# The first tile of W_v loaded and split in two halves of columns

## The chip, the cores and the metric

The kernel runs on one core of a Trainium2 chip. The metric is the device time of one execution in microseconds: before the change 311.23 us, the median of three runs that lie between 311.21 and 311.30 us. Its engines work side by side and wait for each other by semaphores: PE (matmul; its weight loads are listed apart as PEld), DVE and ACT (element-wise work), POOL, and SP, which here does nothing but issue loads and stores. Data move over 16 DMA engines that all queues share.

## The reference, cut to what matters

```
h = rms_norm(x, pre_g)                          # x: (1, 1024, 1024) float32
p = h @ W_in                                    # -> u_A | v_A | g_A | z_B | g_B, 512 columns each
A = gelu(u_A) * (W_s layer_norm(gelu(v_A)) + b_s) * silu(g_A)
B = fourier_mix(z_B) * silu(g_B)                # 2-D DFT over positions and channels, then W_f
y = concat[A, B] @ W_out
out = x + rms_norm(y, post_g)
```

The change touches only the start of the part `v = h @ W_v`, the product of x (scaled by pre_g; the row norm is applied later) with the second 512 columns of W_in.

## The kernel before, in words

float32 operands are kept accurate by splitting: every operand is written as a high part of reduced precision (type fp32r) plus the rest, and a product is three matmuls, high x high, low x high (of the weight's rest), high x low (lines 75 to 78, `mm3`). So a tile has to be loaded, its high part cast (ACT or DVE), and its low part subtracted (DVE) before the third matmul of a product can run. x comes transposed: `hh[kt]` and `hl[kt]` are high and low part of 128 input features (index kt, 0 to 7) by 1024 positions; `wvh`, `wvl` are those of the 128 x 512 tile kt of W_v. A chunk c is 128 positions; its product over all kt is accumulated in one PSUM bank `pv`. Seven chunks run together, tile kt after tile kt.

Loads are issued by SP one after the other in the order of the code: `head0` (138 KB: the gain vectors and the first 256 positions of x's tile 0), `wv0` (256 KB: tile 0 of W_v), `head` (384 KB: the other 768 positions of x's tile 0), then for kt = 1 the tile of W_v (line 125, written `wv`) and the tile of x (`xr1`, 512 KB, line 117; SP's list has the tile of W_v first), then kt = 2 and on.

Before any data are there, PE runs eight matmuls on a tile of ones (`warm`, lines 105 and 106), to be busy when the first product comes. Tile 0 is done by an own loop (lines 235 to 238) in three groups of chunks (0 and 1, 2 to 4, 5 and 6), since the chunks of x arrive in parts; within a group all matmuls of one term run, then those of the next. From kt = 1 on each chunk runs its three matmuls in turn (`v_step`, lines 239 to 241). PE executes in exactly the order of the code. The order on DVE, ACT and SP is made by the scheduler.

DVE casts tile 0 of W_v (line 72) and subtracts for its low part (73), makes the low part of x (135, three slices for tile 0), then does the same for tile 1; ACT makes the high part of x (134) and from tile 1 on also the high part of W_v (70).

Of the kernel before, what the change touches and what calls it, by code (L numbers as in the profile page):

```python
# [15 lines left out]
D = 1024  # L16
KT = D // P
EPS = 1e-6
WARM = 8
LOAD_HALF = 1  # L20
FOLD_AT = (0, 1, 3, 4, 5, 7, 8, 10)
WZ_AT = (2, 6)
# [8 lines left out]
def encoder_layer_kernel(  # L31
# [15 lines left out]
    nc = tc.nc  # L47
# [9 lines left out]
    def slot(name, shape=(P, 1024), dt=F32):  # L57
        return big.tile(list(shape), dt, tag="S", name=name, bufs=NS)
# [6 lines left out]
    def bank(name):  # L65
        return ps.tile([P, 512], F32, tag="ps", name=name)

    def split(src, hi, lo, hi_on_act=True):
        if hi_on_act:
            nc.scalar.copy(hi, src)  # L70
        else:
            nc.vector.tensor_copy(hi, src)
        nc.vector.tensor_tensor(lo, src, hi.bitcast(F32), op=ALU.subtract)  # L73

    def mm3(o, lh, ll, rh, rl, start, stop, **kw):
        nc.tensor.matmul(o, lh, rh, start=start, stop=False, **kw)  # L76
        nc.tensor.matmul(o, lh, rl, start=False, stop=False, **kw)  # L77
        nc.tensor.matmul(o, ll, rh, start=False, stop=stop, **kw)  # L78


    head = slot("head")
    wv0 = raw_slot("wv0")
    head0 = con.tile([P, 276], F32, name="head0")
    vec_sb = head0[:, 0:20]
    nc.sync.dma_start(head0, x0[:, 0:276])
    nc.sync.dma_start(wv0[:, 0:512], w_nat[1, 0])
    nc.sync.dma_start(head[:, 256:1024], x0[:, 276:1044])
    pre_g, ln_g, b_f, ln_b = (vec_sb[:, a:b] for a, b in ((0, 8), (8, 12), (12, 16), (16, 20)))

    ones = con.tile([P, P], F32, name="ones")  # L90
# [13 lines left out]
    warm = bank("warm")  # L104
    for i in range(WARM):
        nc.tensor.matmul(warm[:, 0:P], ones, ones, start=True, stop=True)
# [3 lines left out]
    hh, hl, wv = [], [], []  # L110
    wvh = quad("wvh", (P, 8, 512), F32R)
    for kt in range(KT):
        if kt == 0:
            xr, pg = head, pre_g[:, 0:1]
        else:
            xr = raw_slot(f"xr{kt}")
            nc.sync.dma_start(xr, xT[kt - 1])
            pg = pre_g[:, kt:kt + 1]
        if kt % 2 == 0:
            wr = wv0 if kt == 0 else raw_slot(f"wv{kt}")  # L120
            wv.append((wvh[:, kt:kt + 2], slot(f"wvl{kt}", (P, 2, 512), F32R)))
        wrv = wr.rearrange("p (k n) -> p k n", k=2)[:, kt % 2]
        wh, wl = (t[:, kt % 2] for t in wv[-1])
        if kt > 0:
            nc.sync.dma_start(wrv, w_nat[1, kt])
        h = slot(f"hh{kt}", dt=F32R)
        l = slot(f"hl{kt}", dt=F32R)
        hh.append(h)
        hl.append(l)
        if kt == 0:  # L130
            split(wrv, wh, wl, hi_on_act=False)
        for sl in ([slice(0, 256), slice(256, 640), slice(640, 1024)] if kt == 0 else [slice(0, 1024)]):
            src = head0[:, 20:276] if kt == 0 and sl.start == 0 else xr[:, sl]
            nc.scalar.activation(h[:, sl], src, AF.Copy, scale=pg)
            nc.vector.scalar_tensor_tensor(l[:, sl], src, pg, h[:, sl].bitcast(F32), op0=ALU.mult, op1=ALU.subtract)  # L135
        if kt > 0:
            split(wrv, wh, wl)

    def chunk(t, c):
        return t[:, c * P:(c + 1) * P]  # L140
# [40 lines left out]

    def v_step(pv, c, kt):
        wh, wl = (t[:, kt % 2] for t in wv[kt // 2])
        mm3(pv, chunk(hh[kt], c), chunk(hl[kt], c), wh, wl, kt == 0, kt == KT - 1)


    wz = []
# [44 lines left out]
        return wh, wl  # L232

    pvs = [bank(f"pv{c}") for c in range(7)]
    for cs in (range(2), range(2, 5), range(5, 7)):
        for term in range(3):
            for c in cs:
                nc.tensor.matmul(pvs[c], chunk((hl if term == 2 else hh)[0], c), wv[0][term == 1][:, 0], start=term == 0, stop=False)
    for kt in range(1, KT):
        for c in range(7):  # L240
            v_step(pvs[c], c, kt)
    with tc.manual_schedule(engines={mybir.EngineType.Activation}):
        stats()
        wq = [feature_load(0)]
        wz_load(0)
        const_load()
        for c in range(7):
            v_gelu(c, pvs[c])
        wq.append(feature_load(1))
        v_norm(0, 7)  # L250
        pv = bank("pv7")
        for kt in range(KT):
            v_step(pv, 7, kt)
        v_gelu(7, pv)
        v_norm(7, 8)
# [567 lines left out]
```

## Time and profile before

| | |
|---|---|
| median of the runs | 311.23 us |
| the profiled execution, its own time | 310.65 us |
| its span, first to last instruction | 308.6 us |
| PE busy | 301.3 us, 98% of the span |
| DVE, ACT, POOL busy | 229.8, 131.4, 22.9 us |
| moved by DMA | 42.42 MB, mean 137 GB/s |

The span leaves out 2.05 us of the profiled execution's own time, which lie around the program. An engine's busy time says little about who sets the end; for that there is the chain that ended last, which is followed back from the last instruction to whatever released each step, and the list of waits by engine. Matmuls are pipelined and their ends are modelled, so distances are read from start to start. In timelines "x2" joins neighbours of one kind; in brackets stands the idle time of the engine before a row and what ended it.

### The profile page before, as it was taken

What the parts mean: (1) busy time and instruction counts of PE and PEld (TensorE: products, weight loads), DVE (VectorE), ACT (ScalarE), POOL (GpSimd) and SP (SyncE); (2) the same over time, 40 slices, a digit from 0 to 9 for tenths busy, and PEclk for the clock granted to TensorE, in tenths of its full rate; (3) what the DMA queues carried; (4) which work ended last, traced back from release to release, by engine and by line L of the source; (5) the groups of instructions that cost most, each with busy time, mean ns of one, the idle gap of its engine ahead of it and who ended that gap; (6) DMA issues with size and microseconds to landing.
All of it is one profiled execution on the core that took longest, in us unless ns stands there. A gap on an engine that the chain in (4) does not pass through costs nothing.

```text
span 308.6 us, 3982 instructions
## 1 busy us (share of the span) xinstructions
PE 301.3 (98%) x1497; PEld 253.0 (82%) x1497; DVE 229.8 (74%) x429; ACT 131.4 (43%) x215; POOL 22.9 (7%) x29
## 2 busy tenths in 40 slices
PE   8999999999999999999999999999999999999992
PEld 7788888888888888888888888888888888888881
DVE  4880652579888989987345799655888898898764
ACT  4879476323231233243241334334555554433321
POOL 0000301010000000000000000001310302030210
PEclk9999999999999999999999999999999999999997
DMA  7999716024224151140020108326990163749373
GB/s 248 414 407 410 268 60 204 11 68 135 71 68 138 68 204 55 68 136 2 0 69 2 68 0 213 130 68 194 241 239 10 23 115 67 205 72 265 142 199 143
DMA packets 15427, 42.42 MB, mean 137 GB/s; under 512 B 1456, under 2 KB 1712, under 8 KB 15408
## 3 DMA queue, kind: packets, MB, share of 16 engines
q1 hardware_dynamic: 12880, 35.87, 32.9%
q0 software_dynamic: 2528, 6.30, 11.3%
q8 instruction: 12, 0.20, 0.3%
q14 instruction: 7, 0.06, 0.1%
HBM read 37.96 MB, written 4.20 MB: 137 GB/s over the span
## 4 chain that ended last, share of the span: by engine, by line
PE 95%; DMA 2%; DVE 1%; SPq 1%; ACT 0%; DVEq 0%; POOLq 0%; issue 0%; ACTq 0%
PE pf L77 14%; PE pf L76 14%; PE pf L78 14%; PE pz L285 7%; PE pv L78 4%; PE pv L77 4%; PE pv L76 4%; PE bb L78 4%; PE bb L76 4%; PE bb L77 4%; PE bc L78 2%; PE bc L77 2%; PE bc L76 2%; PE pg L442 2%; PE ba L76 2%; PE ba L78 2%
## 5 line engine op out<-in xcount | busy, mean ns | idle before, releaser
L78 PE MATMUL pv<-wvh,hl 128*128 128x512 f32 x57 | 22.6, 396 | 0.1
L77 PE MATMUL pv<-wvl,hh 128*128 128x512 f32 x57 | 22.5, 394 | 0.0
L70 ACT CAST fh<-sd 128x1024 fp32r<-128x1024 f32 x8 | 8.4, 1049 | 33.0 <-DVE sd L273 33.0
L76 PE MATMUL pv<-wvh,hh 128*128 128x512 f32 x57 | 22.4, 393 | 0.0
L458 ACT ACTIVATE t<-t 128x512 f32<-128x512 f32 x16 | 10.1, 631 | 24.5 <-DVE t L457 24.4
L541 POOL DMA_DIRECT2D wo<-in_w_out x6 | 7.2, 1210 | 174.8 <-DVE t L457 150.9
L457 DVE TENSOR_TENSOR t<-pf,R 128x512 f32<-128x512 f32 x16 | 11.0, 688 | 11.8 <-PE pf L78 11.7
L285 PE MATMUL pz<-wzh,fh 128*128 128x260 f32 x64 | 18.1, 283 | 0.0
L285 PE MATMUL pz<-wzh,fl 128*128 128x260 f32 x64 | 18.0, 281 | 0.0
L285 PE MATMUL pz<-wzl,fh 128*128 128x260 f32 x64 | 18.0, 281 | 0.0
L575 ACT CAST cq<-s 128x512 fp32r<-128x512 f32 x16 | 9.9, 619 | 16.9 <-DVE s L567 15.4
L657 ACT ACTIVATE jk<-y 128x512 f32<-128x512 f32 x12 | 7.6, 632 | 18.6 <-DVE y L730 7.0
L271 DVE TENSOR_TENSOR sd<-hs 128x384 f32<-128x384 f32 x16 | 14.5, 907 | 0.2
L73 DVE TENSOR_TENSOR fl<-sd,fh 128x1024 fp32r<-128x1024 f32 x8 | 9.8, 1224 | 5.2 <-ACT fh L70 5.1
L78 PEld LDWEIGHTS pv<-wvh,hl 128*128 128x128 f32 x57 | 10.7, 188 | 3.0 <-DVE hl L135 0.6
L77 PEld LDWEIGHTS pv<-wvl,hh 128*128 128x128 f32 x57 | 10.7, 188 | 2.5
L76 PEld LDWEIGHTS pv<-wvh,hh 128*128 128x128 f32 x57 | 10.7, 188 | 2.5
L451 ACT ACTIVATE mixA<-t 128x512 f32<-128x512 f32 x8 | 5.1, 632 | 18.1 <-DVE t L450 18.1
L450 DVE TENSOR_TENSOR t<-pf,R 128x512 f32<-128x512 f32 x8 | 5.5, 688 | 9.5 <-PE pf L78 9.5
L285 PEld LDWEIGHTS pz<-wzl,fh 128*128 128x128 f32 x64 | 12.1, 189 | 0.3
L285 PEld LDWEIGHTS pz<-wzh,fh 128*128 128x128 f32 x64 | 12.1, 189 | 0.3
L285 PEld LDWEIGHTS pz<-wzh,fl 128*128 128x128 f32 x64 | 12.1, 189 | 0.0
(383 smaller groups left out, 938.2 us busy)
## 6 DMA issues: line engine op xcount, KB each, us to landing
wo<-in_w_out SPq DMA_DIRECT2D x10, 512.0 KB, 4.6
xc<-in_x SPq DMA_DIRECT2D x8, 512.0 KB, 10.1
xr<-in_xT SPq DMA_DIRECT2D x7, 512.0 KB, 7.7
hs<-in_xT SPq DMA_DIRECT2D x7, 512.0 KB, 3.3
wo<-in_w_out POOLq DMA_DIRECT2D x6, 512.0 KB, 9.0
y<-in_x POOLq DMA_DIRECT2D x5, 512.0 KB, 5.2
out<-y SPq DMA_DIRECT2D x5, 512.0 KB, 3.0
wv<-in_w_nat SPq DMA_DIRECT2D x8, 256.0 KB, 7.0
```

The lines of the kernel that those rows point to most:

```text
L70: nc.scalar.copy(hi, src)
L73: nc.vector.tensor_tensor(lo, src, hi.bitcast(F32), op=ALU.subtract)
L76: nc.tensor.matmul(o, lh, rh, start=start, stop=False, **kw)
L77: nc.tensor.matmul(o, lh, rl, start=False, stop=False, **kw)
L78: nc.tensor.matmul(o, ll, rh, start=False, stop=stop, **kw)
L271: nc.vector.tensor_tensor(sd[:, i, 1:4], hv[:, 1:4], hv[:, 7:4:-1, ::-1], op=op)
L285: nc.tensor.matmul(pz[t][:, cs], l[:, i, t], r[:, cs], start=kt == 0 and i == 0 and j == 0, stop=kt == KT - 1 and i == 1 and j == 2, skip_ ...
L457: nc.vector.tensor_tensor(t, pf, R[:, sl], op=ALU.mult)
L458: nc.scalar.activation(t, t, AF.Silu)
L541: nc.gpsimd.dma_start(t, quarter(add, i), accum_op=ALU.add)
L575: nc.scalar.copy(t[:, 0], src)
L657: nc.scalar.activation(jk[:, 0:w], src, AF.Square, accum_out=ssq[c][:, j:j + 1])
```

## The change

`wv0` is loaded by two DMAs of 256 columns each and the rest of x's tile 0 by two DMAs of 256 and 512 columns, so that five loads stand where three stood. DVE casts and subtracts the first half of the W_v tile as before; the second half is cast by ACT and subtracted by DVE, after the first slice of x. The slices of x's tile 0 become 256, 256 and 512 columns (before 256, 384, 384). PE starts with chunks 0 and 1 by halves of W_v's columns, twelve matmuls of 256 columns; the groups after it are chunks 2 and 3, then 4 to 6. Six warming matmuls run in place of eight.

```diff
-WARM = 8
+WARM = 6
...
-    nc.sync.dma_start(wv0[:, 0:512], w_nat[1, 0])
-    nc.sync.dma_start(head[:, 256:1024], x0[:, 276:1044])
+    for c0 in (0, 256):
+        nc.sync.dma_start(wv0[:, c0:c0 + 256], w_nat[1, 0, :, c0:c0 + 256])
+    for c0, c1 in ((256, 512), (512, 1024)):
+        nc.sync.dma_start(head[:, c0:c1], x0[:, 20 + c0:20 + c1])
...
-            split(wrv, wh, wl, hi_on_act=False)
-        for sl in ([slice(0, 256), slice(256, 640), slice(640, 1024)] if kt == 0 else [slice(0, 1024)]):
+            split(wrv[:, 0:256], wh[:, 0:256], wl[:, 0:256], hi_on_act=False)
+        for sl in ([slice(0, 256), slice(256, 512), slice(512, 1024)] if kt == 0 else [slice(0, 1024)]):
             src = head0[:, 20:276] if kt == 0 and sl.start == 0 else xr[:, sl]
+            if kt == 0 and sl.start == 256:
+                split(wrv[:, 256:512], wh[:, 256:512], wl[:, 256:512])
...
-    for cs in (range(2), range(2, 5), range(5, 7)):
+    for term, half in ((0, 0), (1, 0), (0, 1), (2, 0), (1, 1), (2, 1)):
+        ws = slice(256 * half, 256 * half + 256)
+        for c in range(2):
+            nc.tensor.matmul(pvs[c][:, ws], chunk((hl if term == 2 else hh)[0], c), wv[0][term == 1][:, 0, ws], start=term == half == 0, stop=False, skip_group_check=True)
+    for cs in (range(2, 4), range(4, 7)):
```

SP's list from the start of the program, before (L85 to L87 are tile 0, L125 and L117 the tiles kt = 1 of W_v and x):

```order
L85 DMA head_69<-in_x 128x276
L86 DMA wv_68<-in_w_nat 128x512
L87 DMA head<-in_x 128x768
L125 DMA wv_68<-in_w_nat 128x512
L117 DMA xr_102<-in_xT 128x1024
```

and after the change (L127 and L119 are the old L125 and L117):

```order
L85 DMA head_69<-in_x 128x276
L87 DMA wv_68<-in_w_nat 128x256 x2
L89 DMA head<-in_x 128x256
L89 DMA head<-in_x 128x512
L127 DMA wv_68<-in_w_nat 128x512
L119 DMA xr_104<-in_xT 128x1024
```

The load of x's tile 1 moves from the fifth to the seventh place; what follows it is in the old order.

PE's list from the first product on, before (pv_186 and pv_187 are the banks of chunks 0 and 1):

```order
L238 MATMUL pv_186<-wvh,hh_92 128x512
L238 MATMUL pv_187<-wvh,hh_92 128x512
L238 MATMUL pv_186<-wvl_91,hh_92 128x512
L238 MATMUL pv_187<-wvl_91,hh_92 128x512
L238 MATMUL pv_186<-wvh,hl_93 128x512
L238 MATMUL pv_187<-wvh,hl_93 128x512
```

and after it (the same banks are now pv_188 and pv_189):

```order
L242 MATMUL pv_188<-wvh,hh_92 128x256
L242 MATMUL pv_189<-wvh,hh_92 128x256
L242 MATMUL pv_188<-wvl_91,hh_92 128x256
L242 MATMUL pv_189<-wvl_91,hh_92 128x256
L242 MATMUL pv_188<-wvh,hh_92 128x256
L242 MATMUL pv_189<-wvh,hh_92 128x256
L242 MATMUL pv_188<-wvh,hl_93 128x256
L242 MATMUL pv_189<-wvh,hl_93 128x256
L242 MATMUL pv_188<-wvl_91,hh_92 128x256
L242 MATMUL pv_189<-wvl_91,hh_92 128x256
L242 MATMUL pv_188<-wvh,hl_93 128x256
L242 MATMUL pv_189<-wvh,hl_93 128x256
```

Six matmuls of 512 columns have become twelve of 256; fifteen of 512 columns follow, as before. From tile 1 on PE's list is the same in both, and so are those of DVE, ACT, SP and POOL after their first rows.

## Rows read from the trace of the kernel before

**Rows 1.** The page: the chain that ended last, shares of the span by engine.

```profile
PE 95%; DMA 2%; DVE 1%; SPq 1%; ACT 0%; DVEq 0%; POOLq 0%; issue 0%; ACTq 0%
```

**Rows 2.** Chain that ended last, to 12 us: start, length, engine and line.

```profile
0.74 0.37 SPq L85
...
1.17 0.42 SPq L86
...
1.64 0.42 SPq L87
...
2.58 5.20 DMA xr<-in_xT
...
7.80 1.16 ACT hh L134
...
8.98 1.29 DVE hl L135
...
10.32 0.50 PE pv L78
10.82 0.23 PE pv L76
```

**Rows 3.** Waits of PE's weight loads, whole span: total us, times, longest.

```profile
PEld warm L106 <- DVE ones L91: 1.1, 1, 1.1
PEld pv L78 <- DVE hl L135: 0.6, 1, 0.6
PEld pv L238 <- DVE wvl L73: 0.2, 1, 0.2
```

**Rows 4.** Timeline of PE, three stretches: start, length, line, tiles, count.

```profile
1.06 3.75 PE L106 MATMUL warm<-ones 128*128 128x128 f32 x16 [1.06 <-DVE ones L91]
4.49 0.78 PE L238 MATMUL pv<-wvh,hh 128*128 128x512 f32 x2
...
6.10 0.86 PE L238 MATMUL pv<-wvh,hh 128*128 128x512 f32 x3
...
9.80 0.39 PE L77 MATMUL pv<-wvl,hh 128*128 128x512 f32 x1
...
66.74 1.95 PE L442 MATMUL pg<-wsTb,v 128*128 128x128 f32 x16
68.44 0.48 PE L76 MATMUL pf<-hh,wf1h 128*128 128x512 f32 x1
```

**Rows 5.** Timeline of ACT and of DVE at the start, and one DVE row of the tail.

```profile
2.88 0.51 ACT L134 ACTIVATE hh<-head 128x256 fp32r<-128x256 f32 x1 [0.55 <-DMA head<-in_x]
...
6.38 0.62 ACT L70 CAST wvh<-wv 128x512 fp32r<-128x512 f32 x1
7.80 2.41 ACT L134 ACTIVATE hh<-xr,head 128x1024 fp32r<-128x1024 f32 x2 [0.81 <-DMA xr<-in_xT]
...
3.86 0.43 DVE L72 CAST wvh<-wv 128x512 fp32r<-128x512 f32 x1 [2.86 <-DMA wv<-in_w_nat]
...
8.98 1.28 DVE L135 SCALAR_TENSOR_TENSOR hl<-xr,head,hh 128x1024 fp32r<-128x1024 f32 x1 [1.20 <-ACT hh L134]
...
302.21 0.42 DVE L662 TENSOR_TENSOR yo<-ba,pg_sb 128x256 f32<-128x256 f32 x1
```

**Rows 6.** Stretches: length, busy by engine, granted clock, DMA share, GB/s.

```profile
2.00:3.00 1.00, 1.00 (x7) 1.00 (x6) 0.00 (x0) 0.44 (x3) 0.00 (x0) 1.00 0.96 300
5.00:6.00 1.00, 1.00 (x6) 0.77 (x5) 0.54 (x3) 0.78 (x2) 0.00 (x0) 1.00 1.03 326
```

**Rows 7.** DMA packets of 1.5 to 2.28 us (`head0` alone): count; share of 16 engines.

```profile
DMA packets 90, 0.10 MB, mean 127 GB/s; under 512 B 0, under 2 KB 90, under 8 KB 90
q1 hardware_dynamic: 90, 0.10, 47.0%
```

**Rows 8.** The same of 2.6 to 3 us (`wv0` alone).

```profile
DMA packets 62, 0.13 MB, mean 317 GB/s; under 512 B 0, under 2 KB 0, under 8 KB 62
q1 hardware_dynamic: 62, 0.13, 100.3%
```

More of the change, by code (lines that the diff above doesn't have):

```diff
@@ L183, in v_step @@
         wh, wl = (t[:, kt % 2] for t in wv[kt // 2])
-        mm3(pv, chunk(hh[kt], c), chunk(hl[kt], c), wh, wl, kt == 0, kt == KT - 1)
+        mm3(pv, chunk(hh[kt], c), chunk(hl[kt], c), wh, wl, kt == 0, kt == KT - 1, skip_group_check=c < 2)
     wz = []
```

## The prediction

> **What bounds the kernel now.** I read the chain that ended last first, by engine and then in order of time, since a kernel with PE at 98% can only be moved where PE waits. The chain is PE for 95% of the span [rows 1], so nearly all of it is matmuls in a row; what can be won or lost lies where that row begins. There the chain runs through SP's issues, the load of x's tile 1, the ACT cast of its high part, the DVE subtraction of its low part, and reaches PE at 10.32 us [rows 2]. Tile 0 of W_v, which the change speeds up, isn't in it. Next I read the waits of PE's weight loads over the whole span, to see whether PE waits again later: there are three, all of the start, and the one with the 0.6 us is that at 10.32 us [rows 3]. So the end is the time of `hl` of tile 1 plus a fixed stretch of matmuls.
>
> Then the timeline of PE, to see how far ahead PE was. The second matmul of tile 1 starts at 9.80 us, and matmuls of 512 columns follow each other by 0.23 us (the step of the chain at 10.82 us is that long [rows 2]), so the third could have begun at 10.03 us; it began at 10.32 us [rows 4]. PE stands 0.29 us, and any lead that it gets before that place is waited away in it.
>
> Last the two engines and the load in the chain. ACT had done its cast of W_v's tile 1 at 6.38 + 0.62 = 7.00 us and sat 0.81 us until x's tile 1 had landed; DVE sat 1.20 us for ACT [rows 5]. So that load, issued at 2.58 us and landed 5.20 us later, decides [rows 2].
>
> **The change part by part.**
>
> *PE's start.* The first product waits for the DVE cast of W_v's tile 0, which starts with its landing at 3.86 us and takes 0.43 us; the product follows 0.20 us after it, at 4.49 us [rows 4, 5]. Half of the tile lands earlier: a packet of 2 KB (a row of 512 columns) costs a DMA engine 1.003 x 16 x 0.4 us / 62 = 104 ns [rows 8], one of 1.1 KB 0.470 x 16 x 0.78 us / 90 = 65 ns [rows 7]. With 128 rows on 16 engines, half a tile takes 8 x 39 ns = 0.31 us less, so it lands at about 3.55 us. A DVE cast of 256 columns isn't in the trace: between half of 0.43 us and all of it; I take 0.3 us, nearer to the half, since the low part of 256 columns takes 0.42 us [rows 5]. First product at 3.55 + 0.3 + 0.2 = 4.05 us, a lead of 0.44 us (0.53 us at most, with the cast at 0.21 us). Tile 0 is still 12 half and 15 whole matmuls, 21 x 0.23 = 4.83 us; before, the first six took 6.10 - 4.49 = 1.61 us [rows 4], 0.23 us above 6 x 0.23, for the wait on the low part; I keep 0.25 us for the like. With two matmuls of tile 1, 0.46 us, PE is ready for the third at about 9.6 us in place of 10.03 us. It then waits for `hl` of tile 1, 0.4 us longer. Worth: nothing, as long as that load doesn't come earlier.
>
> *Two fewer warming matmuls.* Sixteen instructions took 4.49 - 1.06 = 3.43 us, 0.214 us each [rows 4]; twelve end at 3.63 us, before the first product can start. Cost nothing, hidden by the wait for the half tile, if the clock rises as before (below).
>
> *More work on ACT and DVE.* ACT gets a cast of 256 columns (under the 0.62 us of 512), hidden by its 0.81 us of waiting; DVE loses a cast of 256 columns and splits a subtraction, one instruction more, hidden by its 1.20 us [rows 5]. The cast waits on ACT for the second half tile; behind it stand the slices of x's tile 0, which are loaded after that half anyway. If their slack were gone, each tenth would go straight into the end.
>
> *The loads, the only part on the path.* x's tile 1 has the same bytes before it, in two DMAs more. Two prices:
> By issue: SP takes 1.64 - 1.17 = 0.47 us per issue [rows 2], so this load is issued 0.94 us later, and so are the tiles behind it, for which PE doesn't wait now [rows 3]. If its landing follows its issue, the end is 0.94 us later. Against that: from 2 us on the DMA engines are at a share of 0.96 to 1.03 [rows 6], so the load waits behind bytes already queued, and its 5.20 us to landing, against at most 2.88 - 0.74 = 2.1 us for `head0`, issued at 0.74 us and awaited by ACT until 2.88 us [rows 2, 5], is mostly queueing.
> By packets: 128 rows of 2 KB become 256 of 1 KB, 8 x (2 x 65 - 104) = 0.21 us per engine; rows of 3 KB become 1 KB and 2 KB, by the line through both prices (145 ns for 3 KB) 8 x (65 + 104 - 145) = 0.19 us. That is 0.40 us above, if the 65 ns, measured while the queue started up, hold; zero below, if a packet costs by its bytes alone. I take 0.2 us, the middle, and keep 0 and 0.94 us as ends.
>
> The Trainium skill, page "DMA: Bandwidth & Descriptors", section "Why small descriptors are slow (HBM only)", gives a fixed overhead of about 3 cycles per packet; at the 850 MHz that it gives for the fabric, 16 more packets per engine would be an estimate of 0.06 us, and the sum 0.14 us lower. The rows here (39 ns less for 0.94 KB less) leave 20 ns that don't go with bytes, so they lean to more than the page has.
>
> *Sum*, against the profiled execution's own 310.65 us: 0 (PE's lead) + 0 (warming) + 0 (ACT, DVE) + 0.2 (packets) = 310.85 us. The median of the runs is 0.58 us above the profiled execution, so on that scale 311.43 us; I forecast 311.4 us.
>
> **The rivals.**
>
> *PE's own start decides in the timed runs.* The profiled execution has the PE 0.29 us ahead of `hl`; the timed runs are 0.58 us longer, and I can't see where. If that lies in PE's first products, PE comes last there, and the change's lead is worth up to its 0.44 us: 311.23 - 0.44 = 310.8 us. For it: the 0.58 us. Against: the chain shown goes through the load.
>
> *The load follows its issue*: 311.23 + 0.94 = 312.2 us, slower. It decides as soon as the DMA engines run empty between the small loads: a half tile is 8 x 65 ns = 0.52 us of work against 0.47 us of issue, so it is close. Against: the shares above.
>
> *The clock rises later*, slower. The warming matmuls come 0.214 us apart, the same shape later 1.70 us / 16 = 0.106 us (66.74 to 68.44 us) [rows 4]: they run at the lower level, 1.2 GHz, though the clock column of that stretch reads 1.00 [rows 6], and the products from 6.10 us on, at 0.23 us, at 2.4 GHz. Before, the warming row runs up to the first product; now PE stands from 3.63 to 4.05 us. If the level rose only halfway through tile 0's products, 10.5 x 0.23 = 2.4 us would be added, PE would be ready at 12.0 in place of 10.32 us: 311.23 + 1.7 = 312.9 us. It decides from the point where PE loses more than the 0.9 us that it will wait at `hl`. Against: behind the 0.29 us for which PE stands at 10.03 us the matmuls still come 0.23 us apart [rows 2].
> The Trainium skill, page "TensorE: Matmul & The Clock Gate", section "Part 1: The HAM clock gate (the "warmup" mystery)", says that the engine starts throttled and that sustained activity releases it; the trace agrees (0.214 against 0.106 us), and by that rule a gap ahead of the first product speaks against the change.
>
> **How the numbers follow.** Forecast 0.70, PE's start 0.17, issue 0.08, clock 0.05. No change is what lies within 0.2%, 0.62 us, of 311.23 us, about what a measurement of this kernel can tell: the forecast (311.2 to 311.7 us, its packets from 0 to 0.4 us) lies inside, and so does the first rival, but for a part that I put at 0.04, where the lead is larger than worked out. The other two are slower: 0.13. So faster 0.04, same 0.83, slower 0.13. The range reaches from the first rival, 310.7 us, to 311.9 us, a little above the forecast's own end and towards the issue rival.
>
> **What would show it.** In the changed profile the chain still goes over x's tile 1, ACT, DVE to the third matmul of tile 1; the first product starts near 4.05 us; the wait of the weight load there grows from 0.6 us to about 1 us or more; the tile lands at 7.8 to 8.2 us in place of 7.78 us; behind it all is shifted by that difference. A landing at 8.7 us shows the issue rival, half matmuls some 0.2 us apart up to 6 us the clock. The forecast is wrong if that landing comes more than 0.1 us earlier, or if the end moves without it.

## The result: slower by 0.6%

| | before | after |
|---|---|---|
| median of the runs of one session | 311.22 us (8 runs, 310.75 to 311.58) | 313.04 us (8 runs, 312.13 to 314.32) |
| the profiled execution, its own time | 310.65 us | 314.08 us |
| its span | 308.6 us | 312.0 us |

The ratio is 1.006 (95% interval 1.0045 to 1.0075). The forecast of 311.4 us and its range, up to 311.9 us, are missed. A second session with the same kernel gave 312.48 us (12 runs, 311.35 to 315.89; ratio 1.0058, 1.0034 to 1.0082).

The chain of waits after the change, in order of time (start, length, engine and line), answers to [rows 2]. ACT's and DVE's rows have line numbers four higher than before, SP's two.

```profile
3.06 0.43 SPq L127
...
3.53 6.23 DMA xr<-in_xT
...
9.78 1.16 ACT hh L138
...
10.96 1.30 DVE hl L139
...
12.30 0.66 PE pv L78
12.96 0.43 PE pv L76
13.39 0.43 PE pv L77
...
15.52 0.43 PE pv L76
15.95 0.26 PE pv L77
```

The places are the same as before. The load of x's tile 1 is issued 0.95 us later (3.53 against 2.58 us), and it also takes 1.03 us longer (6.23 against 5.20 us): it lands at 9.76 us in place of 7.78 us. ACT and DVE take as long as before, so the third matmul of tile 1 starts at 12.30 in place of 10.32 us, 1.98 us later. That matmul takes 0.66 us (0.50 us before), and behind it seven follow at 0.43 us in place of 0.23 us and one at 0.26 us: this is the lower level of PE's clock, 1.2 GHz (the granted clock from 13 to 15 us is 0.50). It costs 0.16 + 7 x 0.20 + 0.03 = 1.6 us. 1.98 + 1.6 = 3.6 us, of which the span shows 3.4 us; the rest was gained back somewhere later and isn't traced.

PE's timeline after (start, length, line, tiles, count; in brackets idle time and what ended it) answers to [rows 4].

```profile
1.06 2.93 PE L108 MATMUL warm<-ones 128*128 128x128 f32 x12 [1.06 <-DVE ones L93]
3.76 0.77 PE L242 MATMUL pv<-wvh,hh 128*128 128x256 f32 x2
4.33 0.63 PE L242 MATMUL pv<-wvl,hh 128*128 128x256 f32 x2
...
5.18 0.61 PE L242 MATMUL pv<-wvh,hl 128*128 128x256 f32 x2
5.61 0.42 PE L242 MATMUL pv<-wvl,hh 128*128 128x256 f32 x2
...
6.10 0.63 PE L246 MATMUL pv<-wvh,hh 128*128 128x512 f32 x2
...
8.89 0.85 PE L246 MATMUL pv<-wvh,hl 128*128 128x512 f32 x3
10.98 0.50 PE L76 MATMUL pv<-wvh,hh 128*128 128x512 f32 x1 [1.24 <-ACT hh L138]
11.31 0.40 PE L77 MATMUL pv<-wvl,hh 128*128 128x512 f32 x1
12.30 0.66 PE L78 MATMUL pv<-wvh,hl 128*128 128x512 f32 x1 [0.59 <-DVE hl L139]
```

PE starts 0.73 us earlier than before (3.76 against 4.49 us) and has tile 0 behind it at 8.89 + 3 x 0.23 = 9.58 us. Then it has nothing to do: it stands for the high part of x's tile 1 and again for the low part. The weight loads, whole span (total us, times, longest), say the same; before, the one wait on the low part was 0.6 us [rows 3].

```profile
PEld pv L76 <- ACT hh L138: 1.7, 1, 1.7
...
PEld pv L78 <- DVE hl L139: 1.0, 1, 1.0
```

### The profile page after: what moved, and what is told of

It reads as the page before. It is cut to its first block, busy times and chain, and to the rows that moved or that the text cites. A ratio compares the mean times of both kernels' runs of the same rounds, so it can differ in the third digit from the quotient of the medians.

```text
span 312.0 us, 3992 instructions
## 1 busy us (share of the span) xinstructions
PE 303.2 (97%) x1499; PEld 254.5 (82%) x1499; DVE 229.8 (74%) x430; ACT 131.9 (42%) x216; POOL 22.9 (7%) x29
## 4 chain that ended last, share of the span: by engine, by line
PE 94%; DMA 2%; SPq 1%; DVE 1%; ACT 0%; DVEq 0%; issue 0%; POOLq 0%; ACTq 0%
PE pf L77 14%; PE pf L78 14%; PE pf L76 14%; PE pz L293 7%; PE pv L78 5%; PE pv L76 4%; PE pv L77 4%; PE bb L78 4%; PE bb L76 4%; PE bb L77 4%; PE bc L77 2%; PE bc L78 2%; PE bc L76 2%; PE pg L450 2%; PE ba L76 2%; PE ba L78 2%
## 5 line engine op out<-in xcount | busy, mean ns | idle before, releaser
L76 PE MATMUL pv<-wvh,hh 128*128 128x512 f32 x57 | 23.2, 407 | 1.2 <-ACT hh L138 1.2
```

## The experiments

All were timed in five rounds beside the kernel before, whose median in its sessions lay at 311.17 (e1 to e4), 311.35 (e5 to e8), 311.28 (e9 to e12), 311.39 (e13 to e16) and 311.11 us (e17, e18). A ratio is the time over that of before, with its 95% interval; where the interval holds 1, no difference is shown. The numbers are the order in which they ran; they stand here by question. "Landing" is that of x's tile 1 in the one profiled execution of each: 7.78 us before, 9.76 us after. PE "stands" where it waits with nothing to do.

### Which part of the change: the loads or the computing

e9: the kernel before with only the loads of the change; the casts, products and eight warming matmuls as before.

```diff
-    nc.sync.dma_start(wv0[:, 0:512], w_nat[1, 0])
-    nc.sync.dma_start(head[:, 256:1024], x0[:, 276:1044])
+    for c0 in (0, 256):
+        nc.sync.dma_start(wv0[:, c0:c0 + 256], w_nat[1, 0, :, c0:c0 + 256])
+    for c0, c1 in ((256, 512), (512, 1024)):
+        nc.sync.dma_start(head[:, c0:c1], x0[:, 20 + c0:20 + c1])
```

> The kernel before with the change's five loads alone: the tile of W_v and the rest of x's tile 0 come in two DMAs each; splits, slices, eight warming matmuls and products are those of the kernel before. Theory L (the loss sits in the landing of x's tile 1, through issues and packets): nearly all of the loss, 312 to 313 us. Theory C (the loss sits in PE's start: a gap behind fewer warming matmuls, half products, and what the clock makes of them): 311.2 to 311.7 us, the sum of the two earlier runs on issues and packets at most.

e10: the reverse, the rest of the change on the three loads of before (ACT's order held as in the changed kernel).

```diff
-WARM = 8
+WARM = 6
...
+            split(wrv[:, 0:256], wh[:, 0:256], wl[:, 0:256], hi_on_act=False)
...
+    for term, half in ((0, 0), (1, 0), (0, 1), (2, 0), (1, 1), (2, 1)):
```

> The other half of the change: the loads of the kernel before (the tile of W_v whole), but its halves cast, subtracted and multiplied as in the changed kernel, with six warming matmuls. Theory L: 311.2 us or a little less. Theory C: 312 us or more, with a spread of 2 us.

e9 took 312.29 us, 1.0 us over before (ratio 1.0034, 1.0022 to 1.0046), e10 311.18 us, no difference (1.0003, 0.999 to 1.0015). The chain of e9:

```profile
3.53 6.32 DMA xr<-in_xT
9.87 1.16 ACT hh L136
11.05 1.30 DVE hl L137
12.39 0.50 PE pv L78
12.90 0.23 PE pv L76
```

With nothing but the loads changed the landing is at 9.85 us, as late as after the whole change, and PE's matmuls behind the stand follow at 0.23 us: the loads bring the late landing, without the fall of the clock. The chain of e10 no longer goes through x's tile 1 (which landed at 7.57 us): it is PE in a row from the first product on.

```profile
3.87 0.41 ACT wvh L70
4.31 2.54 PE pv L244 x12
6.85 3.48 PE pv L248 x15
10.33 0.24 PE pv L76
```

So the halved casts and products bring nothing that can be measured, and cost no more than 0.15%, the end of the interval. The loads alone cost 1.0 us of the 1.2 us (e12) to 1.8 us that the whole change costs; what is above that is taken up below, under the clock.

### What about the loads: issue, packets, or their number

e1: the kernel before with two more issues ahead of tile 1's loads, each of next to no bytes.

```diff
+    tiny = con.tile([P, 16], F32, name="tiny")
+    for i in range(2):
+        nc.sync.dma_start(tiny[0:16, 8 * i:8 * i + 8], x0[0:16, 0:8])
```

> The kernel before with two tiny loads more (16 rows of 32 bytes each, into a tile nobody reads) between the load of x's tile 0 and the loads of tile 1; everything else, the eight warming matmuls and the whole tile of W_v, as before. Theory I (issue): x's tile 1 is issued 0.94 us later and lands as much later; the time is about 312.1 us, that of the quickest runs of the changed kernel, and some runs lie 1 to 2 us above. Theory P (small packets): no packets were cut, so 311.2 us. Theory C (PE's start and its clock): PE's start is untouched, so 311.2 us.

e2: the kernel before with its three loads, but in packets of 1 KB and 1.5 KB: the halves of W_v's tile 0 lie apart in memory, the rest of x in two rows of 384 columns.

```diff
-    nc.sync.dma_start(wv0[:, 0:512], w_nat[1, 0])
+    nc.sync.dma_start(wv0[:, 0:512].rearrange("p (k n) -> p k n", k=2), w_v0.rearrange("k p n -> p k n"))
```

> The kernel before with the same three loads at the start, but the tile of W_v is moved in 256 packets of 1 KB and the rest of x's tile 0 in 256 packets of 1.5 KB, in place of 128 of 2 KB and 128 of 3 KB. Theory P: the packet cost of the change without its issues, 0.4 us or more on x's tile 1, 311.6 to 312.2 us. Theory I: 311.2 us. Theory C: 311.2 us.

e1: 311.35 us (ratio 1.001, 0.9997 to 1.0023), landing at 8.64 us, 0.86 us later. e2: 311.68 us (1.0019, 1.0011 to 1.0028), landing at 7.92 us, 0.14 us later; in its profile the chain is PE in a row from the start and the load isn't in it. In the medians e1 costs 0.18 us, which its interval doesn't tell from nothing, and e2 0.51 us.

One landing is a weak measure, though. Four other versions on this page have the three loads of before untouched, and there x's tile 1 landed at 7.57 us (e10), 8.14 us (e17), 8.45 us (e18) and 8.67 us (e16). ACT's row of e16, which starts 0.02 us behind the landing:

```profile
8.69 2.38 ACT L138 ACTIVATE hh<-xr,head 128x512 fp32r<-128x512 f32 x3 [1.56 <-DMA xr<-in_xT]
```

So the same three loads spread over 1.1 us, and e1's 8.64 us lies within that. The five loads in the order of after landed at 9.59 to 10.10 us in five profiles (after, e9, e11, e12, e15) and at 8.76 us in one (e3): all six later than all five with the three loads, which is why the whole effect is clear where its parts aren't. Then each of the two split loads by itself:

e13: the kernel before with only the W_v lines of e9's edit. e14: with only its x lines.

> The kernel before with only tile 0 of W_v loaded in two halves (four loads where three stood, x's tile 1 in sixth place); casts, products and warming as before. The loads alone (all five) cost 1.0 us and landed x's tile 1 at 9.85 us. Theory A, each load ahead costs its share: half of it, landing at 8.7 to 8.9 us, 311.8 us. Theory B, the halves of W_v do it (their work per engine is about as short as SP's issue, so engines run empty between them): landing near 9.7 us, 312.2 us. Theory C, the parts of x do it: landing at 7.8 to 8.0 us, 311.3 us.

> The kernel before with only the rest of x's tile 0 loaded in two parts of 256 and 512 columns (four loads where three stood); the rest as before. Theory A, each load ahead costs its share: landing of x's tile 1 at 8.7 to 8.9 us, 311.8 us. Theory B, the halves of W_v do it: landing at 7.8 to 8.0 us, 311.3 us. Theory C, the parts of x do it: near 9.7 us, 312.2 us.

e13 landed at 8.44 us (0.66 us later) and took 311.48 us (1.0015, 0.9999 to 1.0031); e14 landed at 8.72 us (0.94 us later) and took 311.99 us (1.0014, 1.0002 to 1.0026). Both are near what theory A forecast, 8.7 to 8.9 us, and far from the 9.7 us of B and C; but 8.44 us lies within the spread of the unchanged loads and 8.72 us 0.05 us above it, so that the landings don't show the share of each load. The rates in the rows further down fit theory A as well. The two medians lie 0.1 and 0.6 us above before, while the ratios are alike, so the times don't say which of them costs more. In e14 PE waits before it comes to tile 1, for the second slice of x's own tile 0, whose load landed at 6.43 us (one wait of PE's weight loads):

```profile
PEld pv L239 <- ACT hh L135: 0.9, 1, 0.9
```

That wait is one more place where a load behind another issue comes late; e9 has the same one, of 1.0 us.

What the DMA engines do meanwhile: the packets that began from 6 to 8 us, first line their count, MB and rate, second the share of the 16 engines' time. Before:

```profile
DMA packets 205, 0.76 MB, mean 380 GB/s; under 512 B 18, under 2 KB 18, under 8 KB 205
...
q1 hardware_dynamic: 205, 0.76, 97.1%
```

After:

```profile
DMA packets 156, 0.58 MB, mean 289 GB/s; under 512 B 14, under 2 KB 14, under 8 KB 156
...
q1 hardware_dynamic: 156, 0.58, 89.7%
```

e9:

```profile
DMA packets 158, 0.56 MB, mean 282 GB/s; under 512 B 16, under 2 KB 16, under 8 KB 158
...
q1 hardware_dynamic: 158, 0.56, 94.4%
```

The packets of this stretch are of the same kind in before and after (3.7 KB each, 0.76 MB / 205 and 0.58 MB / 156). Before, one takes 0.971 x 16 x 2 us / 205 = 152 ns on average; after, 184 ns; in e9, 191 ns. So in this stretch the engines are busy for nearly as much of the time, and move a quarter less. Over the whole stretch from 2 to 8 us (length, busy by engine, clock, DMA share, GB/s), before, after, e9, e1, e2, e13 and e14 in turn:

```profile
2.00:8.00 6.00, 6.00 (x29) 5.22 (x28) 3.43 (x7) 2.77 (x7) 0.00 (x0) 1.00 1.00 335
```
```profile
2.00:8.00 6.00, 6.00 (x31) 5.61 (x30) 3.24 (x8) 3.00 (x7) 0.00 (x0) 1.00 0.91 280
```
```profile
2.00:8.00 6.00, 5.40 (x25) 4.32 (x24) 2.61 (x6) 2.46 (x6) 0.00 (x0) 1.00 0.91 277
```
```profile
2.00:8.00 6.00, 6.00 (x28) 5.04 (x27) 3.11 (x7) 2.57 (x6) 0.00 (x0) 1.00 0.92 300
```
```profile
2.00:8.00 6.00, 6.00 (x24) 5.28 (x23) 2.91 (x6) 2.52 (x7) 0.00 (x0) 1.00 1.00 337
```
```profile
2.00:8.00 6.00, 6.00 (x27) 5.26 (x26) 3.12 (x6) 2.47 (x6) 0.00 (x0) 1.00 0.90 305
```
```profile
2.00:8.00 6.00, 5.14 (x24) 3.95 (x23) 2.35 (x5) 2.31 (x6) 0.00 (x0) 1.00 0.94 309
```

The last two numbers of each row are what to read. The five profiles with the three loads of before (before, e10, e16, e17, e18) have shares of 0.96 to 1.02 and 319 to 346 GB/s. More issues at the same bytes (e1) lower both, to 0.92 and 300 GB/s: the engines run empty for a part of the time. Smaller packets in three loads (e2) lower neither. One load split (e13, e14) gives 305 and 309 GB/s, both split (after, e3, e9, e11, e12, e15) 261 to 280 GB/s at shares of 0.90 to 0.96. So each split lowers the rate. In after the engines are busy for 0.91 of the time, but move 0.84 of the bytes of before.

The part of the bytes that the share doesn't account for sits in a few packets. Read packet by packet, the traces have the middle one (the median) of the packets from 6 to 8 us at 159 ns in before, e1, e2, after and e9 alike. But four packets of after and four of e9 took over 1 us each; they make 4.7 of the 28.7 us and 4.9 of the 30.2 us for which the engines were busy there, and without them the averages are 158 and 165 ns. None of the five profiles with the three loads has such a packet in this stretch, nor have e1, e2, e13 and e14; the other four with the five loads in this order have two (e3) to eight (e15). (Ahead of 6 us one to three turn up in e2, e14, e17 and e18 too.) What holds these packets up isn't settled, and that they hold up the landing isn't shown: e3 has the loads of after, two such packets here and two just ahead of 6 us, and 274 GB/s, and yet its tile 1 landed as long after its issue as before the change.

```profile
3.52 5.23 DMA xr<-in_xT
```

The order of issue was tried too. e4 had ACT issue `head0` in the kernel before (six warming matmuls); e7 held SP to the order of the code, x's tile 1 ahead of W_v's, in the kernel before; e8 the same in the changed one.

```diff
-    nc.sync.dma_start(head0, x0[:, 0:276])
+    nc.scalar.dma_start(head0, x0[:, 0:276])
```

> The kernel before with its first load (the gains and the first 256 positions of x) issued by ACT in place of SP, and six warming matmuls, since the first tile of W_v then comes 0.47 us earlier. All loads behind it are issued 0.47 us earlier. Theory I: x's tile 1 lands up to 0.47 us earlier, PE is ready at about 9.6 us, so the time is 310.8 to 311.0 us. Theory P (bytes and packets decide the landing): 311.2 us.

> The kernel before with SP's loads of the tiles in the order x, W_v (before: W_v first for tile 1); x's tile 1 has 256 KB less in front of it. Theory I (its landing sets the start): it lands some 0.5 us earlier and PE no longer waits for its low part; the quickest runs are 0.3 us under those of before, the median 310.9 us or less. Theory R (the timed runs are mostly set by the time at which PE's clock rises): the median stays at 311.2 us.

> The changed kernel with the same swap of loads. Theory I: x's tile 1 is issued 0.47 us earlier than in the changed kernel and has 256 KB less in front; the stand of PE shrinks to some 0.5 us, the clock does not fall, and the time is 311.0 us or less, under the kernel before, since PE starts 0.5 us earlier. Theory P (small packets at the start slow the queue as a whole): it stays above 311.7 us.

e4: 311.53 us (1.0022, 1.0003 to 1.0042); x's tile 1 was issued at 2.11 us, 0.47 us earlier, and landed at 8.05 us. Its time says nothing of the loads: six of its twelve runs spend 2.3 to 3.5 us outside the span from first to last instruction, where every other run on record spends 2.0 to 2.2 us, and its median span, 309.0 us, is that of before in the same session, 309.1 us. e7: 311.86 us (1.0014, 1.0005 to 1.0023), issued at 2.11, landed at 8.01 us. Both landings lie within the spread of the unchanged loads: an issue 0.47 us earlier shows no gain, and no loss either. e8: 312.19 us (1.0029, 1.0013 to 1.0046); landed at 7.88 us. But in e7 and e8 PE then waited 1.2 us for the low part of W_v's tile 1. The two tiles trade places; the bytes are the same.

### What PE's longer stand costs: the clock

e3: the changed kernel with five warming matmuls between tile 0 and tile 1, in the time in which PE stands. e11: the changed kernel with eight warming matmuls at the start. e12: the changed kernel again.

```diff
+    for i in range(5):
+        nc.tensor.matmul(warm[:, 0:P], ones, ones, start=True, stop=True)
```

> The changed kernel with five more warming matmuls (1.07 us at full clock) on PE between the products of tile 0 and of tile 1, where PE stands. Theory S (the spread of 312.1 to 314.3 us comes from PE standing there, after which the clock falls for a while): the runs gather near 312.2 us and their spread falls to that of the kernel before, some 0.5 us. Theory L (the spread comes from the load landing at different times): the median stays near 313 us or rises a little, spread 2 us.

> The changed kernel with eight warming matmuls in place of six: no gap ahead of the first product, which starts at 4.5 us as before the change. Theory L: as the changed kernel, 313 us (PE has time to spare at x's tile 1). Theory C: about 312 us, with a spread near that of the kernel before.

> The changed kernel once more, for a second profile and more runs beside the others. Theory L: x's tile 1 lands 0.8 us or more later than before in this profile too. Theory C: it may land at about 8 us, and PE loses time at the lower clock instead.

e3: 312.06 us (1.0035, 1.0022 to 1.0048); e11: 312.27 us (1.0039, 1.002 to 1.0058); e12: 312.48 us. In their profiles the landings are at 8.76, 9.72 and 10.10 us, and the matmuls behind the stand follow at 0.23 us in all three. The waits of e12:

```profile
PEld pv L76 <- ACT hh L138: 1.4, 1, 1.4
...
PEld pv L78 <- DVE hl L139: 1.0, 1, 1.0
```

Those of e11 are the 1.7 and 1.0 us of after again. So a stand of the same length is followed by the lower level of the clock in one execution and not in the other. The fall was seen in one profile of the six that have the five loads and a stand left open (after, e8, e9, e11, e12, e15).

The timed runs have no trace, but the record gives the mean granted clock of each. In all 147 runs of before that have one it is 0.993 to 0.999; the profiled execution of after, with its fall, has 0.990. Of all runs on record six lie below 0.993, all of them above 314 us: two of the eight of after, three of the twelve of e12 and one of e8. So about a quarter of the runs of the changed kernel seem to have had a fall; that a low mean is a fall at this place is an inference from the one trace. Without these runs the medians are 312.56 us (after, six runs) and 312.34 us (e12, nine runs), near the 312.29 us of e9, in which no run is that low. A long run isn't always a fall: e11 has one of 314.12 us at 0.996.

Whether e3's fill keeps the clock up or only had an early landing can't be told from its 312.06 us. Eight warming matmuls in place of six change nothing that these intervals can tell.

e5 and e6 put four tiny loads ahead of tile 1's loads in the kernel before (x's tile 1 then went ahead of W_v's), e6 with eight warming matmuls in the stand as well.

> The kernel before with four tiny loads (16 rows of 32 bytes) between the load of x's tile 0 and those of tile 1, where SP's list now has x's tile 1 ahead of W_v's: tile 1 comes about 1.4 us late, and PE stands some 2 us in the middle of an otherwise unchanged start. Theory S (a stand of this length lets PE's clock fall for a while): more than the delay itself is lost, 313 to 314.5 us, with a spread of 2 us. Theory L (only the landing counts): the delay alone, about 312.5 us, spread as before.

> The same with eight warming matmuls (1.7 us at full clock) on PE between the products of tile 0 and of tile 1, in the time in which PE stands. Theory S: 0.8 us or more less than without them, about 312.3 us, with little spread. Theory L: the same time as without them or a little more.

e5: 311.96 us (1.0016, 1.0008 to 1.0025), a stand of 1.0 us and no fall of the clock; e6: 312.46 us (1.0037, 1.0023 to 1.005), its eight matmuls being longer than the stand, so that they were on the path. They didn't tell the clock's part apart.

### Is the path behind the landing what counts

e15: the changed kernel with the parts of x's tile 1 made in two slices of 512 positions. e16: the same in e10. e17: the same in the kernel before, alone. e18: e16 again.

```diff
-        for sl in (... if kt == 0 else [slice(0, 1024)]):
+        for sl in (... if kt == 0 else [slice(0, 512), slice(512, 1024)] if kt == 1 else [slice(0, 1024)]):
```

> The changed kernel with the high and low part of x's tile 1 made in two slices of 512 positions, so that the third product of chunk 0 needs half of ACT's 1.16 us and of DVE's 1.30 us behind the landing. Theory, the late landing and the two steps behind it are the path: that product starts some 1.2 us earlier behind the same landing (about 1.3 us behind it in place of 2.54 us), and the time falls by about 1.2 us, to 311.3 to 311.8 us, the stand of PE being short too. Rival, the loss lies elsewhere (PE's early stand and the clock): PE waits as long, 312.5 us or more.

> The halved casts and products and six warming matmuls on the three loads of before, with the high and low part of x's tile 1 in two slices of 512 positions. Theory: with the old landing (7.6 to 7.9 us) the low part of the first half is there by 9.2 us, before PE has done tile 0, so PE never stands at tile 1 and its own start decides; that start was 0.2 us earlier than before, so 311.0 to 311.2 us, no more than 0.3 us under before. Rival, tile 1's wait decided in most runs of before and is gone now: 310.6 us.

> The kernel before with one edit: the high and low part of x's tile 1 in two slices of 512 positions. Theory, the wait for tile 1 decided part of the runs of before and the slices take it away: the same gain as the version with halved products and slices (0.17%, 310.8 us). Rival, the gain of that version needs PE's earlier start as well: with the slices alone PE only loses the 0.29 us for which it stood in the profile of before, 311.0 to 311.3 us.

> The version with halved casts and products, six warming matmuls and two slices of x's tile 1 on the three loads of before, run a second time (0.17% under before in the first): theory, 310.6 to 311.0 us again, under before by 0.1 to 0.25%; rival, the first was a draw of lucky executions and this one ties with before, 311.2 us or more.

e15: 311.52 us (ratio to before 1.0007, 0.9993 to 1.0021), 1.0 to 1.5 us below the changed kernel's two medians. Its chain:

```profile
3.53 6.06 DMA xr<-in_xT
...
9.61 0.73 ACT hh L138
10.34 0.02 issue
10.36 0.76 DVE hl L139
...
11.17 0.50 PE pv L78
11.67 0.23 PE pv L76
```

The landing is as late (9.59 us), but the product that needs it starts 1.58 us behind it in place of 2.54 us, and the time falls by about as much. That shows the path. No run of e15 has a mean granted clock below 0.994, so a part of the gain may be falls of the clock that didn't come.

e16: 310.81 us (0.9983, 0.9973 to 0.9993); e18, the same kernel: 310.61 us (0.9991, 0.9981 to 1.0001); e17: 310.75 us (0.9993, 0.9984 to 1.0002). So the version with slices on the old loads is the fastest tried, 0.1 to 0.2% below before, in one session clear of no change and in the other at its edge; e17 leaves it open whether the earlier start of PE adds anything to the slices.

## Why the prediction was wrong, point by point

- *What bounds the kernel*: right. The chain goes over x's tile 1, ACT and DVE to the third matmul of tile 1 in after and in e9, and e15 gives time back by shortening just that.
- *PE's start, worth nothing*: right. The half tile landed early enough for the first product at 3.76 us (4.05 us forecast); the cast of 256 columns took 0.29 us (0.3 us taken). But the half products ran 0.21 us apart, the lower level, up to 5.6 us, so that tile 0 was done at 9.58 us, where 4.05 + 4.83 + 0.25 = 9.13 us was forecast. Either way the rest was waited away, and e10 alone brings nothing.
- *Warming, ACT and DVE, nothing*: right. ACT sat 2.58 us before it began on x's tile 1 and DVE 2.84 us; e11's eight warming matmuls change nothing measurable.
- *The loads, 0.2 us (0 to 0.94 us)*: this step failed, in its size. The landing came 1.98 us later in the profile, and the loads alone (e9) cost 1.0 us in the median, five times the 0.2 us taken. The prediction set two prices side by side, by packets or by issue, and took the first because the DMA engines showed shares of 0.96 to 1.03 [rows 6], which it read as a queue already full. A share near 1 says only that the queue is full at this pace of issue: two more issues at the same bytes lowered it to 0.92 (e1), the five loads to 0.91, and the rate from 335 to 280 GB/s. The two prices don't exclude each other, and even their sum, 0.94 + 0.40 = 1.34 us, is short of the landing of after. How large each of them is stays open: the landings of e1 (0.86 us later) and e2 (0.14 us later) lie within the spread of the unchanged loads, 7.57 to 8.67 us. By that spread the sign named for the issue rival, a landing at 8.7 us, couldn't be read from one profile either. What wasn't foreseen are the few packets of over 1 us from 6 to 8 us, which came with the five loads.
  The Trainium skill's page "DMA: Bandwidth & Descriptors", section "Why small descriptors are slow (HBM only)", has a fixed overhead per packet, from which the prediction worked out an estimate of 0.06 us. No run here can show an amount so far below the spread of the landings, and packets of one size that take 159 ns or over 1 us aren't told by it.
- *The rival "the load follows its issue", 312.2 us, 0.08*: nearest to the times (312.3 us in e9, 312.5 and 313.0 us in after), and its condition, engines that run empty between small loads, fits the share of 0.91. That its price is the issue alone isn't shown. It deserved more than 0.08: 0.52 us of work against 0.47 us of issue left next to no margin.
- *The rival of the clock*: it looked at the rise, at the start. That did come later than the first product, but PE's lead covered it. What cost 1.6 us in the profiled execution was a fall, behind a stand that the forecast itself had made longer and had priced at nothing; that the profiled execution was one with a fall is chance, by the granted clocks.
  The Trainium skill's page "TensorE: Matmul & The Clock Gate", section "HAM oscillation — how this bites in real kernels", tells of waits for a DMA behind which the engine starts again at the lower level. The profile of after agrees (0.43 us behind waits of 1.24 and 0.59 us); those of e11, with waits as long, and of e12, with 0.95 and 0.60 us, don't.
- *The rival "PE's own start decides"*: e10's chain, PE in a row from the first product on, shows that it can; but the changed kernel had taken the load's slack away, so it had no say.

## What to carry to other kernels

A load that decides the end should have as few issues ahead of it as possible: splitting what stood before it delayed it here even though the DMA engines looked full, since a share near 1 holds only for the pace at which the loads are issued now. How late a load lands should be read from several profiles: the same loads landed up to 1.1 us apart. An engine's lead that is waited away isn't always free, because PE's stand can be followed by its lower clock level. Where a late tile decides, making its first consumer need only a slice of it (e15; e16 to e18 at the edge of what the intervals tell) was worth more here than loading anything earlier.

## What the runs showed of the hardware

The clock's rise isn't at the same time in every execution. e16 and e18 are one kernel; the twelve half products of the first took 2.70 us, those of the second 1.98 us:

```profile
4.41 2.70 PE pv L244 x12
7.11 3.48 PE pv L248 x15
```
```profile
4.37 1.98 PE pv L244 x12
6.34 3.48 PE pv L248 x15
```

Both began within 0.04 us of each other, and the products behind them take the same 3.48 us, so 0.72 us of the end hang on when the level rises; in the timelines pairs of half products start 0.43 us apart up to 6.69 us in e16, and 0.24 us apart from 5.23 us on in e18. It is as much as the whole effect of many edits here, and may be part of why the times of before spread from 310.4 to 312.4 us over the sessions.
The Trainium skill's page "TensorE: Matmul & The Clock Gate", section "What's actually happening", says that the number of matmuls at the lower level differs from run to run of one kernel; these two profiles agree.

The packets of x's and W_v's tiles from 6 to 8 us took 152 ns on average before and 184 ns after, with no other queue in that stretch. The middle one took 159 ns in both; most of the difference is four packets of over 1 us each. No run here says what holds them up.
